# Moved tile regions, halved products and a re-ordered entry in a hybrid decoder layer

## The chip, the cores and the metric

The kernel runs on one core of a Trainium2 chip. The metric is device time in microseconds (us), as the median of several runs. A core has five engines that work from queues of their own: PE (TensorE, the matrix unit, with its weight loads shown apart as PEld), DVE (VectorE), ACT (ScalarE), POOL (GpSimd) and SP (SyncE, here only an issuer of DMAs). Each engine takes its instructions strictly in order; an instruction that has to wait for another engine or for a transfer holds up all behind it.

## The reference

One decoder layer over 512 tokens of width 1024, all in float32, and a last norm:

```python
h = h + 0.5 * swiglu(rmsnorm(h, ffn1_norm), w_gate, w_up, w_down)      # FFN1, inner width 2816
proj = rmsnorm(h, mix_norm) @ w_in                                     # the mix: gMLP and SSD side by side
h = h + concatenate([ya, yb]) @ w_out
h = h + 0.5 * swiglu(rmsnorm(h, ffn2_norm), w_gate, w_up, w_down)      # FFN2
gate = sigmoid(rmsnorm(h, ple_norm) @ ple_w_gate + ple_b_gate)         # the gate
h = h + gate * (p @ ple_w_proj)                                        # p @ ple_w_proj: the embedding
return rmsnorm(h, final_norm)
```

`swiglu(x) = (silu(x @ w_gate) * (x @ w_up)) @ w_down`. `p` is 512 x 256.

## The kernel before, in words

**A product.** Activations lie with the model width over the 128 partitions and the 512 tokens along the free side; a weight block of 128 x 128 is the stationary operand, the activations are the moving one. To keep float32 accuracy on PE, each operand is split into two float32r parts, a high part (`whi`, `xhi`) cast by ACT (L498 for weights) and a low part (`wlo`, `xlo`), the rest, subtracted by DVE (L502). A product is three matmuls into one bank: whi with xhi, whi with xlo, wlo with xhi (L213, L214, L215 in `passes`). Weights arrive by DMA as `raw`, `rawb`, `raw0` or `rawd`.

**Stages.** In order: the embedding p @ ple_proj (two units, steps 0 and 1, L1010), which is written out to DRAM and read back at the end; FFN1; the mix; the projection out; FFN2; the gate; the final norm and the rows out.

**An FFN** has 22 blocks of 128 of the inner width, in eleven groups of two. Group 0 is computed "plainly": four steps (gate and up, each over a lower and an upper half of the width), whose moving operands are the tiles `xfa` and `xfb`, 48 matmuls of 512 columns for the gate and as many for up, 96 in all. Groups 1 to 10 go by a scheme with seven products of 256 columns in place of eight (L712); some of its weights are sums, which are formed by a DMA from POOL that adds to a tile already loaded (L727 and L730 ahead of product 7, L764 for the weights of product 3). Down (`ghi`, `glo` moving, 512 columns) is done in six parts over one or two groups, with weights in `whi` or, from another region, in `whix`.

**The gate** has eight units of 128 of the width: five whole ones of 24 matmuls of 512 columns each (`accumulate` in the loop at L1759) and the last three (`BY_HALF`) by halves of 256 columns, tokens 0 to 255 first, so that the final norm of one half runs beside the products of the other (`gate_half`, 144 matmuls).

**Places.** Tiles come from a base region and from a left and a right region for each stage. `PAD` gives bytes of padding for each; a left region is padded at its start, a right one at its end, from where it grows downwards. In the built programs the tiles begin at these bytes of a partition, modulo 128:

| tile | before | after |
|---|---|---|
| whi, wlo (base) | 0 | 0 |
| xfa, xfb (FFN, left) | 64 | 64 |
| ghi, glo, whix, wlox (FFN, right) | 96 | 0 |
| x of the mix, ya, yb | 0 | 0 |
| x of the gate (ple, left) | 0 | 64 |

Halves of 256 columns lie 1024 bytes apart and so keep the tile's place. The embedding, too, uses ghi and glo of the right region as moving tiles.

**Order.** The first 18 steps follow `ENTRY`, a list written by hand: loadN issues a step's DMAs, splitN its casts and subtractions, productN its matmuls, afterN what is done with the result; N.1 and N.2 are further chains of the step and ":k" its next k pieces. From it and from fixed rules for the rest come the orders of PE, ACT, DVE and SP. POOL's order is not written down; the scheduler places its instructions. Steps 2 to 5 are the plain ones, step 6 is the first L712 product, step 12 a piece of down, and step 13 a product 3 whose weights `rawb` need L764. Before the first real matmul, `WARM` idle matmuls run (L179).

Of the kernel before, what the change touches and what calls it, by code (L numbers as in the profile page):

```python
# [31 lines left out]
P = 128  # L32
T = 512
NC = T // P
D = 1024
ND = D // P
# [6 lines left out]

D_ORDER = tuple(d + i for d in range(NP) for i in (0, NP))
AHEAD = 6
WARM = 10
BY_HALF = 3
LOADS, MIX_LOADS = 6, 4

ENTRY = """  # L50
load0 load1 load1.1 load2 load3 load3.1 split0 load4 split1:1 load5 split1.1:2 split1 split1.1
load6 load6.1 product0 split2 load7 product1 after0 split3 split3.1:6 split4.1:3 split4.2:1
split4.1:1 split4.2:1 split3.1 load8 product2 split4.2:1 after1 split4 split4.1 split4.2:1
split4.2:1 split6.2:1 split4.2 load9 split6.2:1 product3 split5 split5.1 split6.1 split5.2
after4:1 split5.3 product4 split6 after4 split6.2 product5 after4.1 split7 split7.1 load12
product6 split8:1 after5:1 split8 sums9 after6 after5:2 split9:1 split10:1 split10.1:1 after5
product7 split9 load14 product8 after7 split10 split10.1 split14:1 load15 product9 split11
after8 split14 load16 product10 after9 after10 split12 load17 after10.1:1 product11 after11
split13 after10.1 product12 after+10 after11.1:1 after12:1 after11.1 after11.2 product13
after+11 split15 after12 product14 after13:1 split16 after13  # L60
"""

BUFS = {
# [9 lines left out]

PAD = {"sb": 96, "ffn_left": 256, "mix_left": 320, "ple_left": 320, "ffn_right": 0, "mix_right": 96, "ple_right": 0}
HEADS = 16
HD = 64
GROUPS = 2
# [19 lines left out]
def layer_kernel(ctx: ExitStack, tc: tile.TileContext, a: dict, out: bass.AP):  # L99
    nc = tc.nc  # L100
# [76 lines left out]
    ps = sm_ps()  # L177
    for _ in range(WARM):
        nc.tensor.matmul(ps, idle[:, :P], idle, start=True, stop=True)  # L179
    nc.scalar.copy(vec_warm, ones[:, 0:1])  # L180

    upper = sb("upper", (P, P))
    nc.gpsimd.affine_select(
# [26 lines left out]

    def passes(ps, whi, wlo, xhi, xlo, first, last):

        nc.tensor.matmul(ps, whi, xhi, start=first, stop=False)  # L213
        nc.tensor.matmul(ps, whi, xlo, start=False, stop=False)  # L214
        nc.tensor.matmul(ps, wlo, xhi, start=False, stop=last)  # L215

    def accumulate(ps, w, j0, xs, first=True, last=True, tokens=slice(0, T)):

# [464 lines left out]
    class Group:  # L683
# [94 lines left out]
        def plain_steps(self, first):  # L778


            def step(w, i, which, lower):
                w_parts = {}

                def split():
                    return w.split_by_engine(kept=w_parts)

                def product():
                    whi, wlo = w_parts[0]
                    if not lower:
# [182 lines left out]
    def embedding(q):  # L972
        w = Parts()
        ps = []
        raw = sb("g", (P, 2, T)) if q == 0 else None

        def load():
            if q:
                w.load(a["ple_proj"][q])
                return  # L980
            nc.sync.dma_start(raw[:, 0], a["p"][:, 0])
            w.raw = sb(w.tag, (P, 1024))
            for k in range(2):
                c = slice(k * T, (k + 1) * T)
                nc.sync.dma_start(w.raw[:, c], a["ple_proj"][q][:, c])
            nc.sync.dma_start(raw[:, 1], a["p"][:, 1])
            nc.sync.dma_start(vec, a["vecs"])

        def split():
            if q:  # L990
                yield from w.split_by_engine()
                return
            hi, lo = sb("ghi", (P, 2, T), F32R), sb("glo", (P, 2, T), F32R)
            w.take()
            for k in range(2):
                for t, r, u in ((hi[:, k], raw[:, k], lo[:, k]), (w.hi, w.raw, w.lo)):
                    if r is w.raw:
                        t, r, u = (v[:, k * T : (k + 1) * T] for v in (t, r, u))
                    nc.scalar.copy(t, r)
                    nc.vector.tensor_tensor(u, r, t.bitcast(F32), ALU.subtract)  # L1000
            pe.extend((hi[:, k], lo[:, k]) for k in range(2))

        def product():

            ps.extend(acc_ps() if i == 3 else bank("mm", 3) if q else sm_ps() for i in range(4))
            for k, (xhi, xlo) in enumerate(pe):
                for n, (wt, xt) in enumerate(((w.hi, xhi), (w.hi, xlo), (w.lo, xhi))):
                    for i in range(4):
                        c = slice((4 * k + i) * P, (4 * k + i + 1) * P)
                        nc.tensor.matmul(ps[i], wt[:, c], xt, start=k == n == 0, stop=k == 1 and n == 2)  # L1010

        def out():
            for i, tag in enumerate(("embt", "embt", "p7", "u2", "rawd", "rawd", "rawd", "rawd")[4 * q : 4 * q + 4]):
                if tag in ("p7", "u2") or i % 2 == 0:
                    t = sb(tag, (P, 1 if tag in ("p7", "u2") else 2, T))
                    n = 0
                (nc.vector.tensor_copy if i > 1 else nc.scalar.copy)(t[:, n], ps[i])
# [733 lines left out]
    def done(d, ps):  # L1751
# [4 lines left out]
            nc.gpsimd.tensor_tensor(total, total, sq, ALU.add)  # L1756
        gained(d, whole)

    for d in range(ND - BY_HALF):  # L1759
        ps = mm_ps()  # L1760
        accumulate(ps, weights(a["ple_gate"][d], D), 0, x)
        if d == 0:
            tok, first = norm.per_token(D), ps
            continue
        if d == 1:
            r = Norm.on_all(tok)
            done(0, first)
        done(d, ps)
# [138 lines left out]
```

## Time and profile before

| | us |
|---|---|
| median of 3 runs | 1080.93 (1080.79 to 1082.17) |
| the profiled execution | 1080.79 |
| its span | 1079.1 |
| PE busy in it | 1068.1 |
| first matmul of the embedding | 5.65 |
| first plain product of FFN1 | 16.95 |
| first L712 product | 40.55 |
| step 13's first matmul | 59.68 |
| first plain product of FFN2 | 683.42 |
| first matmul of the gate | 1019.72 |

All times in rows are microseconds from the span's start: when an instruction starts, how long it takes, its engine, line and operation, output <- input, and in brackets how long the engine was idle before it and what ended that. Several instructions can be merged in a row (x2, x3). Matmuls overlap, so that a row's duration is longer than the distance to the next start.

### The profile page before, as it was taken

The page shows a single profiled execution, that of the slowest core. Times are in us where ns is not written, and L with a number is a line of the kernel's source. Part 1 is how long each engine was busy: PE and PEld are TensorE (multiplying, and loading weights), DVE is VectorE, ACT ScalarE, POOL GpSimd, SP SyncE. Part 2 cuts the span into 40 slices and gives each one's busy share as a digit, 9 for nine tenths or more (in the row PEclk, how much of TensorE's full clock was granted, in tenths as well). Part 3 has the DMA queues.
Part 4 walks back from the last instruction along what each step waited for, and adds up shares of the span by engine and source line. Part 5 has one row for each costly group of instructions (what it writes and reads, how often), then busy time and mean ns, then how long its engine had stood idle before and what let it go on. Part 6 is the DMA issues. An engine that isn't in the chain of part 4 may idle for free.

```text
span 1079.1 us, 16531 instructions
## 1 busy us (share of the span) xinstructions
PE 1068.1 (99%) x6679; PEld 946.1 (88%) x6679; DVE 778.9 (72%) x1080; ACT 514.9 (48%) x711; POOL 136.5 (13%) x125
## 2 busy tenths in 40 slices
PE   9999999999999999999999999999999999999997
PEld 7999999999998888787888888899999999999887
DVE  7987676666666786766997756688766677677766
ACT  7644444344444455565754334354444434343554
POOL 0100000000001200043233000000000000000411
PEclk9999999999999999999999999999999999999998
DMA  9997776575523332444432333767756676633412
GB/s 346 287 240 186 193 188 183 157 195 159 135 59 120 95 98 81 143 133 135 129 107 77 98 98 98 218 167 200 213 141 168 184 195 177 179 114 107 144 44 79
DMA packets 49885, 163.77 MB, mean 152 GB/s; under 512 B 5648, under 2 KB 5904, under 8 KB 49808
## 3 DMA queue, kind: packets, MB, share of 16 engines
q1 hardware_dynamic: 39872, 129.09, 35.8%
q0 software_dynamic: 8640, 31.46, 16.8%
q10 hardware_dynamic: 1296, 2.16, 0.6%
q8 instruction: 52, 0.85, 0.3%
q14 instruction: 25, 0.20, 0.1%
HBM read 158.43 MB, written 4.26 MB: 151 GB/s over the span
## 4 chain that ended last, share of the span: by engine, by line
PE 89%; DVE 5%; ACT 2%; DMA 1%; issue 1%; SPq 1%; DVEq 0%; ACTq 0%
PE mm L712 20%; PE a L712 15%; PE sm L214 10%; PE sm L213 10%; PE sm L215 10%; PE mm L214 4%; PE mm L213 4%; PE mm L215 4%; PE a L213 3%; PE a L215 3%; PE a L214 3%; DVE wlo L502 1%; DVE tmp L1731 1%; DMA raw<-in_w_in 1%; DMA h<-in_x 1%
## 5 line engine op out<-in xcount | busy, mean ns | idle before, releaser
L498 ACT CAST whi<-raw 128x1024 fp32r<-128x1024 f32 x138 | 144.2, 1046 | 162.0 <-issue 65.0
L502 DVE TENSOR_TENSOR wlo<-raw,whi 128x1024 fp32r<-128x1024 f32 x137 | 172.0, 1255 | 61.0 <-ACT whi L498 59.6
L712 PE MATMUL mm<-xfb,whi 128*128 128x256 f32 x960 | 166.0, 276 | 0.0
L712 PEld LDWEIGHTS mm<-xfb,whi 128*128 128x128 f32 x960 | 145.8, 188 | 1.6
L712 PE MATMUL mm<-xfb,wlo 128*128 128x256 f32 x480 | 132.6, 276 | 0.0
L215 PE MATMUL sm<-ghi,wlox 128*128 128x512 f32 x296 | 116.3, 393 | 0.0
L214 PE MATMUL sm<-glo,whix 128*128 128x512 f32 x296 | 115.9, 391 | 0.0
L213 PE MATMUL sm<-ghi,whix 128*128 128x512 f32 x296 | 115.2, 389 | 0.0
L712 PE MATMUL a<-xfb,whi 128*128 128x256 f32 x640 | 110.9, 276 | 0.0
L712 PEld LDWEIGHTS a<-xfb,whi 128*128 128x128 f32 x640 | 97.7, 188 | 1.9 <-issue 0.2
L712 PEld LDWEIGHTS mm<-xfb,wlo 128*128 128x128 f32 x480 | 90.1, 188 | 0.0
L712 PE MATMUL a<-xfb,wlo 128*128 128x256 f32 x320 | 88.4, 276 | 0.3 <-DVE wlo L502 0.3
L502 DVE TENSOR_TENSOR wlox<-rawd,whix 128x1024 fp32r<-128x1024 f32 (+1 forms) x40 | 45.7, 1142 | 58.8 <-ACT whix L498 58.8
L502 DVE TENSOR_TENSOR wlo<-rawb,whi 128x1024 fp32r<-128x1024 f32 x52 | 63.6, 1223 | 18.9 <-ACT whi L498 18.9
L855 ACT ACTIVATE g<-g 128x512 f32<-128x512 f32 x40 | 25.3, 632 | 106.6 <-DVE g L853 106.6
L727 POOL DMA_DIRECT2D raw<-in_ffn_gu x20 | 17.3, 865 | 401.4 <-DVE h L911 125.3
L498 ACT CAST whi<-rawb 128x1024 fp32r<-128x1024 f32 x52 | 54.3, 1044 | 28.2 <-DVE rawb L722 17.7
L911 DVE SCALAR_TENSOR_TENSOR h<-sm,h 128x512 f32<-128x512 f32 x96 | 63.2, 685 | 5.2 <-PE sm L215 4.6
L215 PEld LDWEIGHTS sm<-ghi,wlox 128*128 128x128 f32 x296 | 55.5, 188 | 11.7
L213 PEld LDWEIGHTS sm<-ghi,whix 128*128 128x128 f32 x296 | 55.6, 188 | 11.0 <-DVE h L911 0.2
L214 PEld LDWEIGHTS sm<-glo,whix 128*128 128x128 f32 x296 | 55.5, 188 | 10.9
L712 PEld LDWEIGHTS a<-xfb,wlo 128*128 128x128 f32 x320 | 60.1, 188 | 0.5 <-DVE wlo L502 0.5
(423 smaller groups left out, 2488.7 us busy)
## 6 DMA issues: line engine op xcount, KB each, us to landing
raw<-in_ffn_gu SPq DMA_DIRECT2D x56, 512.0 KB, 6.0
rawd<-in_ffn_down SPq DMA_DIRECT2D x40, 512.0 KB, 4.0
rawb<-in_ffn_gu SPq DMA_DIRECT2D x32, 512.0 KB, 5.5
raw<-in_ffn_gu POOLq DMA_DIRECT2D x30, 512.0 KB, 5.6
raw<-in_w_in SPq DMA_DIRECT2D x29, 512.0 KB, 3.7
s<-in_ffn_gu SPq DMA_DIRECT2D x20, 512.0 KB, 7.1
s<-in_ffn_gu POOLq DMA_DIRECT2D x20, 512.0 KB, 8.7
raw<-in_w_out SPq DMA_DIRECT2D x16, 512.0 KB, 3.6
```

Source lines behind the costliest of these rows:

```text
L213: nc.tensor.matmul(ps, whi, xhi, start=first, stop=False)
L214: nc.tensor.matmul(ps, whi, xlo, start=False, stop=False)
L215: nc.tensor.matmul(ps, wlo, xhi, start=False, stop=last)
L498: nc.scalar.copy(self.hi[:, : self.n], self.raw[:, : self.n])
L502: nc.vector.tensor_tensor(self.lo[:, :n], self.raw[:, :n], self.hi[:, :n].bitcast(F32), ALU.subtract)
L712: nc.tensor.matmul(o, wt[:, c], xt, start=fresh and p == m == n == 0, stop=last and n == 2, skip_group_check=True,)
L727: nc.gpsimd.dma_start(w21.raw, self.src[0], accum_op=ALU.add)
L855: nc.scalar.activation(t, t, AF.Silu)
L911: nc.vector.scalar_tensor_tensor(h[d], ps[d], 0.5, h[d], ALU.mult, ALU.add)
L1731: engine.tensor_tensor(t, t, emb[d][:, tok], ALU.mult)
```

## The change

It has six parts.

1. `PAD`: `ffn_right` 0 to 96, which moves every tile of the FFNs' right region down by 96 bytes, and `ple_left` 320 to 256, which moves the gate's x by 64 (table above).
2. The plain products: each matmul of 512 columns becomes two of 256 (`passes` once for each half of the tokens). 96 matmuls in each FFN become 192.
3. The gate's five whole units likewise, in `gate_product`: 120 become 240. PE has 312 matmuls more less one idle one.
4. The embedding: the first half of p is asked for by ACT's queue (before it: SP's), ahead of ACT's table load; the first half of the first unit's weights is cast by DVE (before: ACT); the second unit's matmuls go bank by bank, six for each bank, and not pass by pass over four banks.
5. `WARM` 10 to 9.
6. `ENTRY` is another list.

```diff
-WARM = 10
+WARM = 9
...
-load0 load1 load1.1 load2 load3 load3.1 split0 load4 split1:1 load5 split1.1:2 split1 split1.1
+load0 load1 load1.1 load2 load3 load3.1 load4 load5 split0 split1:1 split1.1:3 split1 split1.1
...
-PAD = {"sb": 96, "ffn_left": 256, "mix_left": 320, "ple_left": 320, "ffn_right": 0, "mix_right": 96, "ple_right": 0}
+PAD = {"sb": 96, "ffn_left": 256, "mix_left": 320, "ple_left": 256, "ffn_right": 96, "mix_right": 96, "ple_right": 0}
...
-    nc.scalar.copy(vec_warm, ones[:, 0:1])
...
-        nc.tensor.matmul(ps, whi, xhi, start=first, stop=False)
-        nc.tensor.matmul(ps, whi, xlo, start=False, stop=False)
-        nc.tensor.matmul(ps, wlo, xhi, start=False, stop=last)
+        for n, (w, x) in enumerate(((whi, xhi), (whi, xlo), (wlo, xhi))):
+            nc.tensor.matmul(
+                ps, w, x, start=first and n == 0, stop=last and n == 2, skip_group_check=True
+            )
...
-                            passes(
-                                by_half(ps), whi[:, c], wlo[:, c], t[:, 0:2, 0], t[:, 0:2, 1],
-                                not lower and p == 0, lower and p == len(self.xfs) - 1,
-                            )
+                            for s in range(2):
+                                passes(
+                                    by_half(ps)[:, s], whi[:, c], wlo[:, c], t[:, s, 0], t[:, s, 1],
+                                    not lower and p == s == 0, lower and p == len(self.xfs) - 1 and s == 1,
+                                )
...
-            nc.sync.dma_start(raw[:, 0], a["p"][:, 0])
+            nc.scalar.dma_start(raw[:, 0], a["p"][:, 0])
+            nc.scalar.copy(vec_warm, ones[:, 0:1])
...
-                for t, r, u in ((hi[:, k], raw[:, k], lo[:, k]), (w.hi, w.raw, w.lo)):
-                    if r is w.raw:
-                        t, r, u = (v[:, k * T : (k + 1) * T] for v in (t, r, u))
-                    nc.scalar.copy(t, r)
+                c = slice(k * T, (k + 1) * T)
+                of_p = hi[:, k], raw[:, k], lo[:, k]
+                of_w = w.hi[:, c], w.raw[:, c], w.lo[:, c]
+                nc.scalar.copy(*of_p[:2])
+                (nc.scalar.copy if k else nc.vector.tensor_copy)(*of_w[:2])
+                for t, r, u in (of_p, of_w):
...
-            for k, (xhi, xlo) in enumerate(pe):
-                for n, (wt, xt) in enumerate(((w.hi, xhi), (w.hi, xlo), (w.lo, xhi))):
-                    for i in range(4):
-                        c = slice((4 * k + i) * P, (4 * k + i + 1) * P)
-                        nc.tensor.matmul(ps[i], wt[:, c], xt, start=k == n == 0, stop=k == 1 and n == 2)
+            order = [(k, n, i) for k in range(2) for n in range(3) for i in range(4)]
+            for k, n, i in sorted(order, key=lambda t: t[2]) if q else order:
+                (xhi, xlo), c = pe[k], slice((4 * k + i) * P, (4 * k + i + 1) * P)
+                wt, xt = ((w.hi, xhi), (w.hi, xlo), (w.lo, xhi))[n]
+                nc.tensor.matmul(ps[i], wt[:, c], xt, start=k == n == 0, stop=k == 1 and n == 2)
...
+    def gate_product(ps, w):
+
+        for k, (xhi, xlo) in enumerate(x):
+            for tok in halves:
+                c = slice(k * P, (k + 1) * P)
+                passes(
+                    ps[:, tok], w[0][:, c], w[1][:, c], xhi[:, tok], xlo[:, tok],
+                    k == tok.start == 0, k == ND - 1 and tok.start > 0,
+                )
+
     for d in range(ND - BY_HALF):
         ps = mm_ps()
-        accumulate(ps, weights(a["ple_gate"][d], D), 0, x)
+        gate_product(ps, weights(a["ple_gate"][d], D))
```

The new lines shift line numbers by up to 14; L764 and L727 stay, L1010 becomes L1014, L1017 becomes L1021.

What stands where, at three places. First POOL, whose DMAs add to tiles already loaded, in groups 1 and 2 of FFN1. `rawb_51` before and `rawb_53` after is the tile of step 13; `raw_125` is a tile of group 2's product 7. Before:

```order
L727 DMA raw_62_220<-in_ffn1_gu 128x1024
L730 DMA s1_63_223<-in_ffn1_gu 128x1024
L764 DMA rawb_51_178<-in_ffn1_gu 128x1024
L727 DMA raw_125_610<-in_ffn1_gu 128x1024
L730 DMA s1_126_613<-in_ffn1_gu 128x1024
L727 DMA raw_162_875<-in_ffn1_gu 128x1024
```

And after:

```order
L727 DMA raw_64_225<-in_ffn1_gu 128x1024
L730 DMA s1_65_228<-in_ffn1_gu 128x1024
L727 DMA raw_125_704<-in_ffn1_gu 128x1024
L764 DMA rawb_53_181<-in_ffn1_gu 128x1024
L730 DMA s1_126_707<-in_ffn1_gu 128x1024
L727 DMA raw_162_970<-in_ffn1_gu 128x1024
```

L764 for step 13 and the L727 of raw_125 have changed places.

Second PE, in the embedding's second unit (step 1), whose four banks are mm, mm, mm and a. Before, from the second row of the unit:

```order
L1010 MATMUL mm_66_229<-ghi_41_148,whi_46_162 128x512
L1010 MATMUL mm_67_230<-ghi_41_148,whi_46_162 128x512
L1010 MATMUL a0_68_231<-ghi_41_148,whi_46_162 128x512
L1010 MATMUL mm_65_228<-glo_42_149,whi_46_162 128x512
L1010 MATMUL mm_66_229<-glo_42_149,whi_46_162 128x512
L1010 MATMUL mm_67_230<-glo_42_149,whi_46_162 128x512
L1010 MATMUL a0_68_231<-glo_42_149,whi_46_162 128x512
L1010 MATMUL mm_65_228<-ghi_41_148,wlo_47_163 128x512
```

After, from the second row of the unit:

```order
L1014 MATMUL mm_67_233<-glo_44_152,whi_47_163 128x512
L1014 MATMUL mm_67_233<-ghi_43_151,wlo_48_164 128x512
L1014 MATMUL mm_67_233<-ghi_43_151,whi_47_163 128x512
L1014 MATMUL mm_67_233<-glo_44_152,whi_47_163 128x512
L1014 MATMUL mm_67_233<-ghi_43_151,wlo_48_164 128x512
L1014 MATMUL mm_68_234<-ghi_43_151,whi_47_163 128x512
```

The first matmul with wlo is the unit's third, where it was its ninth, and the first bank is finished after six matmuls, where it was after 21.

Third ACT, where it empties that unit's first two banks into rawd (L1017, after the change L1021). The xfb casts are operands of the upper plain steps. Before:

```order
L498 CAST whi_72_263<-raw0_40_142 128x1024
L596 ACTIVATE glo_74_267<-h_14_102,vec_2_70 128x512
L596 ACTIVATE glo_75_270<-h_16_104,vec_2_70 128x512
L600 CAST xfb_21_109<-glo_74_267 128x2x512
L600 CAST xfb_23_111<-glo_75_270 128x2x512
L629 CAST xfb_21_109<-ghi_76_275 128x512
L629 CAST xfb_23_111<-glo_77_277 128x512
L629 CAST xfb_21_109<-ghi_76_275 128x512
L1017 COPY rawd_81_314<-mm_65_228 128x512
L1017 COPY rawd_81_314<-mm_66_229 128x512
```

And after:

```order
L1021 COPY embt_73_265<-sm_59_192 128x512
L629 CAST xfb_21_107<-ghi_71_261 128x512
L629 CAST xfb_23_109<-glo_72_263 128x512
L498 CAST whi_76_276<-raw0_40_141 128x1024
L600 CAST xfb_21_107<-glo_62_219 128x2x512
L600 CAST xfb_23_109<-glo_63_222 128x2x512
L1021 COPY rawd_81_337<-mm_67_233 128x512
L1021 COPY rawd_81_337<-mm_68_234 128x512
```

One xfb cast fewer stands ahead of the rawd copies, and the two L596 have gone further forward.

Behind the steps of `ENTRY`, ACT, DVE, SP and POOL have the same order as before.

More of the change, by code (lines that the diff above doesn't have):

```diff
@@ L50 @@
 ENTRY = """
-load0 load1 load1.1 load2 load3 load3.1 split0 load4 split1:1 load5 split1.1:2 split1 split1.1
[L52 to L60, printed above, removed]
+load0 load1 load1.1 load2 load3 load3.1 load4 load5 split0 split1:1 split1.1:3 split1 split1.1
+split2 load6 load6.1 product0 split3.1:4 load7 product1 split4.1:2 after0:2 split4.1:1 after0:1
+split4.1:1 after0 split4.2:2 split3 split3.1:2 split4.1:1 split3.1 load8 product2 after1 split4
+split4.1 split6.2:1 split4.2 load9 product3 split5 split5.1 split5.2 split6.2:1 split6.1
+split6.2:1 after4:1 split5.3 product4 after4 split6 split6.2 product5 after4.1 split7 split7.1
+load12 product6 after5:1 split8 after6 sums9 after5:1 split9:1 after5 product7 split10.1:1
+split9 load14 split10.1:1 product8 split10.1:1 after7 split10 split10.1 split14:1 load15
+product9 split11 after8 load16 product10 after9 split12 load17 product11 split13:1 after10
+after10.1:1 split14 after11 after10.1 split13 product12 after+10 after11.1 after11.2 after12:1
+product13 after+11 split15 after12 split16:1 product14 after13:1 split16 after13
 """
```

## The prediction

> **What bounds the kernel now.** I read the page's busy line, then PE's waits, then PE's instructions in order of time, one stretch for each kind of matmul, and last the queues that feed the first steps.
>
> ```profile
> PE 1068.1 (99%) x6679; PEld 946.1 (88%) x6679; DVE 778.9 (72%) x1080; ACT 514.9 (48%) x711; POOL 136.5 (13%) x125
> PE mm L213 <- ACT rawd L1017: 0.5, 1, 0.5
> PE a L712 <- DVE wlo L502: 0.3, 1, 0.3
> ```
>
> PE works nearly always, and its waits are tenths of a microsecond. So the time is the number of matmuls times their pitch (start to start). Pitch, not the busy time of one row, is what to read, since matmuls overlap. Six stretches give it (start, duration):
>
> ```profile
> 683.42 0.39 PE L213 MATMUL sm<-xfa,whi 128*128 128x512 f32 x1
> 694.62 0.95 PE L275 MATMUL sm<-ones,ssum 128*128 128x1 f32 x8
> 991.99 0.39 PE L712 MATMUL mm<-xfb,whi 128*128 128x256 f32 x2
> 997.43 0.39 PE L213 MATMUL sm<-ghi,whi 128*128 128x512 f32 x1
> 1005.57 0.39 PE L215 MATMUL sm<-ghi,wlox 128*128 128x512 f32 x1
> 1008.06 0.39 PE L214 MATMUL sm<-glo,whix 128*128 128x512 f32 x1
> 1008.52 0.39 PE L213 MATMUL sm<-ghi,whi 128*128 128x512 f32 x1
> 1019.72 0.39 PE L213 MATMUL mm<-x,whi 128*128 128x512 f32 x1
> 1025.31 1.05 PE L275 MATMUL sm<-ones,ssum 128*128 128x1 f32 x8
> 1029.07 0.39 PE L213 MATMUL a<-x,whi 128*128 128x512 f32 x1
> 1031.79 0.62 PE L312 MATMUL sm<-tmp,onesr 128*128 128x512 f32 x2
> 1060.08 0.28 PE L213 MATMUL sm<-x,whi 128*128 128x256 f32 x1
> 1062.96 0.28 PE L1786 MATMUL sm<-ones,ssum 128*128 128x1 f32 x2
> ```
>
> 512 columns: 48 of FFN2's plain matmuls in 694.62 - 683.42 = 11.20 us, 233.3 ns each; 48 of down with whi in 1019.72 - 1008.52 = 11.20, 233.3; 11 of down with whix in 2.49, 226.4; 12 of the gate in 2.72, 226.7. 256 columns: 48 of L712 in 5.44, 113.3; 24 of the gate's halves in 2.88, 120.0. Beside the table of places above, one rule fits all six: with 512 columns the moving tile at the stationary tile's place (modulo 128 bytes) gives the short pitch, another place the long one; with 256 columns it is the other way round, 64 bytes apart is short and 0 is long. The table of places after the change says that every 512 column matmul it touches then lies at 0, and every 256 column one at 64.
>
> The sum is made against the profiled execution: 1080.79 us, a span of 1079.1 and 1.7 around it, 0.14 under the median of the runs, 1080.93. All terms but the first are PE's own work on a PE that is never idle beside it.
>
> **1. The entry, to step 13.** Rows of PE, the queues, DVE and ACT in order of time, a bracket giving the idle time before and what ended it:
>
> ```profile
> 11.35 0.86 PE L1010 MATMUL mm<-ghi,whi 128*128 128x512 f32 x3
> 13.22 0.86 PE L1010 MATMUL mm<-ghi,wlo 128*128 128x512 f32 x3
> 22.31 0.40 PE L215 MATMUL sm<-xfa,wlo 128*128 128x512 f32 x1
> 23.20 0.50 PE L213 MATMUL mm<-xfa,whi 128*128 128x512 f32 x1 [0.49 <-ACT rawd L1017]
> 59.68 0.40 PE L712 MATMUL a<-xfb,whi 128*128 128x256 f32 x2
> 59.91 0.28 PE L712 MATMUL a<-xfb,wlo 128*128 128x256 f32 x1
> 0.81 0.39 SPq L981 DMA_DIRECT2D g<-in_p  x1
> 10.92 1.22 DVE L502 TENSOR_TENSOR wlo<-raw,whi 128x1024 fp32r<-128x1024 f32 x1
> 55.99 1.05 ACT L498 CAST whi<-rawb 128x1024 fp32r<-128x1024 f32 x1 [3.20 <-DMA rawb<-in_ffn_gu]
> 57.69 1.22 DVE L502 TENSOR_TENSOR wlo<-rawb,whi 128x1024 fp32r<-128x1024 f32 x1
> 61.82 1.22 DVE L502 TENSOR_TENSOR wlo<-raw,whi 128x1024 fp32r<-128x1024 f32 x1
> 65.41 0.28 PE L712 MATMUL mm<-xfa,wlo 128*128 128x256 f32 x1
> 47.33 0.84 POOL L764 DMA_DIRECT2D rawb<-in_ffn_gu  x1 [16.84 <-DVE wlo L502]
> 49.97 0.86 POOL L727 DMA_DIRECT2D raw<-in_ffn_gu  x1 [1.79 <-DMA raw<-in_ffn_gu]
> 115.28 0.86 POOL L727 DMA_DIRECT2D raw<-in_ffn_gu  x1 [15.52 <-DMA raw<-in_ffn_gu]
> 116.46 0.85 POOL L730 DMA_DIRECT2D s<-in_ffn_gu  x1 [0.33 <-issue]
> ```
>
> POOL's transfers in the view of DMA issues, which ends with the time from issue to landing: the three from 47 to 54 us, then the two from 115 to 117:
>
> ```profile
> rawb<-in_ffn_gu POOLq DMA_DIRECT2D x1, 512.0 KB, 8.6
> raw<-in_ffn_gu POOLq DMA_DIRECT2D x1, 512.0 KB, 8.6
> s<-in_ffn_gu POOLq DMA_DIRECT2D x1, 512.0 KB, 9.2
> ...
> raw<-in_ffn_gu POOLq DMA_DIRECT2D x1, 512.0 KB, 5.6
> s<-in_ffn_gu POOLq DMA_DIRECT2D x1, 512.0 KB, 6.9
> ```
>
> What PE gains by itself: FFN1's 96 plain matmuls as pairs save 96 x 6.6 ns = 0.63. The hole between 22.31 and 23.20 (0.89 where one pitch is 0.23, so 0.66) mostly closes, since the units' banks are finished one by one and ACT can empty rawd's first ones early. p's issue leaves SP (0.39, so ple_proj is asked for 0.4 earlier; ACT's table load now stands behind an issue instead, and what either is worth lies ahead of the wait below). Against it: the second embedding unit needs wlo at its third matmul and not at its ninth. The first wlo matmul would stand some 0.46 behind the unit's start instead of 13.22 - 11.35 = 1.87, and wlo is ready at 10.92 + 1.22 = 12.14, or a few tenths sooner as ACT's cast comes sooner. That is a new wait of 0.3 to 0.8 that eats the earlier start. I take 0.63 + 0.66 - 0.2 = 1.1 us earlier at step 13, were nothing else in the way.
>
> Something is. Step 13's weights are rawb, to which L764 adds by DMA; ACT's cast waited 3.20 us for that landing, and wlo was ready at 57.69 + 1.22 = 58.91, 1.0 before its first use at 59.91. On POOL, L764 used to stand ahead of the second L727; now it stands behind it, and that L727 waits until 49.97 for its own tile's load, which no edit brings sooner (the SP queue's order is otherwise as before). So L764 is issued at 49.97 + 0.86 = 50.83, not 47.33. When does it land? The pair at 115.28 and 116.46 landed at 120.88 and 123.36: the first took 5.6, the second came 2.5 later. By that L727 lands at 55.57 and L764 at 58.05. The ends: as quick as the second of that pair from its own issue, 50.83 + 6.9 = 57.7, or 0.4 less if raw lands sooner, 57.3; as the second of the two in the run before, 49.97 + 8.6 = 58.6. I take 58.05, which lies between them. Then the cast ends at 58.05 + 0.09 + 1.05 = 59.19 and wlo at 60.42: PE's third matmul of step 13 stands at 60.42, not 59.91. What is queued behind the cast and wlo (silu, h, the next wlo) moves by 1.5 too; the next product is not late by it, for its wlo (61.82 + 1.22 = 63.04) stood 2.4 ahead of its use at 65.41, and PE itself is 0.5 later. So the entry's 1.1 is lost and **+0.51** is paid; ends -0.24 (57.3) and +1.1 (58.6). The 12 aligned down matmuls ahead of step 13 are hidden by the same wait.
>
> **2. FFN1's down, last two groups of blocks:** 24 + 48 matmuls with base whi, 72 x 6.6 = 0.48, less what a block pays to settle: 24 gate matmuls took 1025.31 - 1019.72 = 5.59, 0.15 over 24 x 226.7. **-0.34** (ends -0.48, 0).
>
> **3. FFN2's plain:** 96 matmuls of 233.3 as 192 of 113.3: **-0.63**. No row before has a plain pair; the ends are L712's 113.3 (same xfa and xfb, same kind of weights) and the gate halves' 120.0, which would give 96 x 6.7 = +0.64. I take L712's, the row with the same tiles and the same 64 bytes.
>
> The Trainium skill's "TensorE: Matmul & The Clock Gate", section "Back-to-back issue gap", speaks against splitting: beside its columns each isolated matmul costs 2.5 ns, so a pair costs that much more than one of 512. The trace has two of L712 at 226.7, no more than one aligned matmul of 512. By the page's rule the 216 pairs behind step 13 would add an estimated 0.54, and the sum would be 1079.5.
>
> **4. FFN2's down:** 12 + 24 + 48 matmuls x 6.6 = 0.55, less 0.18 to settle: **-0.37** (ends -0.55, 0).
>
> **5. FFN2's one wait:**
>
> ```profile
> 740.83 0.38 PE L712 MATMUL a<-xfb,wlo 128*128 128x256 f32 x1 [0.35 <-DVE wlo L502]
> 739.55 1.23 DVE L502 TENSOR_TENSOR wlo<-raw,whi 128x1024 fp32r<-128x1024 f32 x1 [1.17 <-ACT whi L498]
> ```
>
> PE comes here 0.70 earlier (terms 3 and 4's first 12). The wlo is the end of a chain through DVE and ACT that is partly fed by PE's own earlier products, so a part of it comes earlier too. **+0.2** (ends 0, +0.70).
>
> **6. The gate's five whole units:** 120 matmuls of 226.7 as 240 of 113.3 cost nothing; the settling of the first two (0.15 and some 0.05) goes: **-0.2**; at 120.0 for a half the end is +1.6.
>
> **7. The gate's halves:** 144 matmuls, 120.0 to 113.3 with x moved: 144 x 6.65 = **-0.96** (end 0). The rest of the tail hangs on PE's end.
>
> Sum: 0.51 - 0.34 - 0.63 - 0.37 + 0.2 - 0.2 - 0.96 = -1.79, so 1080.79 - 1.79 = **1079.0 us**.
>
> **The rivals.**
> B, L764 lands in time. If it lands by 56.4, wlo is there when PE comes 1.1 early, term 1 is -1.1 and the time 1080.79 - 3.4 = 1077.4. For it: the 8.6 of the run before was a loaded time, as the 5.6 and 6.9 of the later pair show. Against: from 50.83 that is 5.6 us, the time of a transfer with nothing ahead of it.
>
> C, places don't set the pitch, and halving costs: the long pitch belongs to these tiles for another reason, and a product cut in two pays what the only cut rows of the gate pay, 2 x 120. Then the moves give nothing, FFN2's plain pays +0.64, the gate +1.60, the entry +0.51: 1080.79 + 2.75 = 1083.5, slower. It decides from a pair price of 227.3 ns on (96 and 120 pairs against 49.6 us now, 0.51 beside them). Against it: xfa and xfb themselves show 113.3 in L712, and one tile, ghi, shows 233.3 with whi and 226.4 with whix, so it is the pair of tiles that counts.
> The Trainium skill's "SBUF — State Buffer", section "Who interferes with whom", says that PE never waits on anyone and reads both operands by ports of their own; by it no place should matter, which is this rival; the two pitches of ghi speak against the page.
>
> D, L764 lands as late as the third of the burst did, 52.55 + 9.2 = 61.8, from POOL's row:
>
> ```profile
> 52.55 0.85 POOL L730 DMA_DIRECT2D s<-in_ffn_gu  x1 [1.72 <-DMA s<-in_ffn_gu]
> ```
>
> Then step 13 is 3.7 later than in my sum: 1082.7. From a landing at 59.8 on the gain is gone. For it: all three of that burst took over 8.5, and L764 would stand in its middle.
>
> **How the numbers follow.** This forecast 0.58, B 0.22, C 0.07, D 0.08, others 0.05. A difference under 0.2%, 2.16 us, can't be told from none: faster means under 1078.8, slower over 1083.1. My own case spreads from 1078.2 (57.3 at step 13) to 1080.2, so some two fifths of it lie under 1078.8: faster 0.24 + 0.22 + 0.02 = 0.48; slower, most of C and a part of D, 0.07; same 0.45. The range goes from B to a landing between mine and D's: 1077.1 to 1081.0.
>
> **What would show it.** L712's pitch unchanged, plain, gate and halves all at 113.3, down at 226.7 everywhere: terms 2 to 7. L764 issued after L727 at about 50.8; ACT's cast of rawb near 58.1; a new PE wait on wlo in step 13 of about 1.6 us. Wrong if plain or gate pairs take 240, if down with whi stays at 233, if L764 lands before 57 or after 60, or if a later wait takes the gains back.

## The result, and the profile after

The changed kernel takes 1092.03 us (median of 4 runs, 1090.82 to 1095.70) against 1080.92 (1080.79 to 1082.17) beside it: a ratio of 1.0106 [1.008, 1.0131], 11.1 us slower where 1.9 faster was forecast. The profiled execution is the slowest of the four, 1095.70 us with a span of 1094.0, so the trace has 14.9 us to explain, 3.7 of which the median run does not have.

From the page of the kernel after, the busy line and one group of matmuls, with that group's line on the page of before under it; then, from the view of waits after, PE's:

```profile
PE 1079.2 (99%) x6990; PEld 972.9 (89%) x6990; DVE 781.0 (71%) x1081; ACT 515.0 (47%) x710; POOL 136.6 (12%) x125
L712 PE MATMUL mm<-xfb,whi 128*128 128x256 f32 x960 | 171.4, 280 | 0.0
L712 PE MATMUL mm<-xfb,whi 128*128 128x256 f32 x960 | 166.0, 276 | 0.0
PE a L712 <- ACT whi L498: 2.8, 1, 2.8
PE a L712 <- DVE wlo L502: 1.1, 2, 0.8
PE sm L1800 <- DVE tmp L1741: 0.8, 1, 0.8
```

PE is still never idle but for a few microseconds, so again it is pitch that has grown. Start times of the same work in the two traces, in us from the span's start, show where:

| | before | after | difference | step of it |
|---|---|---|---|---|
| first plain product of FFN1 | 16.95 | 17.25 | +0.30 | +0.30 |
| first L712 product | 40.55 | 39.59 | -0.96 | -1.26 |
| step 13 | 59.68 | 61.64 | +1.96 | +2.92 |
| the product behind step 13 | 65.18 | 69.87 | +4.69 | +2.73 |
| last L712 product of FFN1 | 327.38 | 337.60 | +10.22 | +5.53 |
| first plain product of FFN2 | 683.42 | 693.22 | +9.80 | -0.42 |
| first L712 product of FFN2 | 707.17 | 717.00 | +9.83 | +0.03 |
| last L712 product of FFN2 | 994.71 | 1009.77 | +15.06 | +5.23 |
| first matmul of the gate | 1019.72 | 1034.36 | +14.64 | -0.42 |
| end of the span | 1079.1 | 1094.0 | +14.9 | +0.26 |

Two things carry it: a slow creep of 5.5 and 5.2 us through the L712 products of both FFNs, and 5.65 us around step 13.

**The creep.** PE's instructions in order of time near the end of FFN2, at the place where the prediction read 48 of L712 in 5.44 us. After:

```profile
1006.26 0.39 PE L213 MATMUL sm<-ghi,whix 128*128 128x512 f32 x1
1006.49 0.39 PE L213 MATMUL sm<-glo,whix 128*128 128x512 f32 x1
1006.72 0.39 PE L213 MATMUL sm<-ghi,wlox 128*128 128x512 f32 x1
1006.94 0.40 PE L712 MATMUL mm<-xfb,whi 128*128 128x256 f32 x2
1007.18 0.28 PE L712 MATMUL mm<-xfb,wlo 128*128 128x256 f32 x1
...
1009.77 0.40 PE L712 MATMUL a<-xfb,whi 128*128 128x256 f32 x2
...
1012.60 0.39 PE L213 MATMUL sm<-ghi,whi 128*128 128x512 f32 x1
```

48 of L712 now take 1012.60 - 1006.94 = 5.66 us, 117.9 ns each and not 113.3, although neither xfa, xfb nor the weights have another address. In the whole trace 3072 of the 3744 matmuls with xfa or xfb and 256 columns are at 118 (counted by products of 24, each by its median pitch). I call the step from the last matmul of down to the first of L712 the hand-over. Down's rows ahead of the same place before, its first ones and its last:

```profile
986.73 0.40 PE L214 MATMUL sm<-glo,whix 128*128 128x512 f32 x1
986.96 0.40 PE L215 MATMUL sm<-ghi,wlox 128*128 128x512 f32 x1
...
991.30 0.39 PE L213 MATMUL sm<-ghi,whix 128*128 128x512 f32 x1
991.53 0.39 PE L214 MATMUL sm<-glo,whix 128*128 128x512 f32 x1
991.75 0.40 PE L215 MATMUL sm<-ghi,wlox 128*128 128x512 f32 x1
```

The difference is in the last 512 column matmul. Before, it is uneven, that is, its pitch is not that of its neighbours: it is 0.40 long and 237 ns from its successor (unrounded), where they have 227. After, it is as even as the rest, 227. The other sign is on the other side of the block: before, down's first matmuls behind L712 are uneven too (986.73, 986.96: 0.40), after they run at 226.7 from the first. What these rows show holds nearly everywhere: the trace of before has 40 hand-overs, and in 37 of them the last pitch is 236 or 237 ns and the product behind it is at 113; after, 37 have 226 or 227 and 118 behind it.

**Step 13.** These are rows of POOL, ACT, DVE and PE in order of time, after:

```profile
50.72 0.84 POOL L727 DMA_DIRECT2D raw<-in_ffn_gu  x1 [20.73 <-DVE wlo L502]
51.26 1.19 POOL L764 DMA_DIRECT2D rawb<-in_ffn_gu  x1
60.54 1.04 ACT L498 CAST whi<-rawb 128x1024 fp32r<-128x1024 f32 x1 [8.71 <-DMA rawb<-in_ffn_gu]
61.62 1.23 DVE L502 TENSOR_TENSOR wlo<-rawb,whi 128x1024 fp32r<-128x1024 f32 x1 [4.81 <-ACT whi L498]
61.64 0.50 PE L712 MATMUL a<-xfb,whi 128*128 128x256 f32 x2 [2.82 <-ACT whi L498]
62.90 0.38 PE L712 MATMUL a<-xfb,wlo 128*128 128x256 f32 x1 [0.76 <-DVE wlo L502]
```

L764's transfer lands 9.2 us after its issue. The issue was late too, since L727 ahead of it waits for the load of its own tile, which landed 7.7 us after its issue at 42.44; the same load took 6.5 us before. L727 goes out 0.55 us behind that landing, as it does in experiments 2 and 10; the DVE instruction in its bracket ended in between. PE waits 2.82 us for whi, does two matmuls, and waits 0.76 for wlo. Then it works at half speed: windows of 2 us, with the granted clock in the column behind the five engines:

```profile
62.00:64.00 2.00, 1.24 (x9) 1.10 (x8) 2.00 (x4) 0.12 (x1) 0.00 (x0) 0.88 1.02 325
64.00:66.00 2.00, 2.00 (x12) 2.00 (x11) 2.00 (x5) 1.92 (x3) 0.00 (x0) 0.50 1.02 418
66.00:68.00 2.00, 2.00 (x11) 1.88 (x11) 2.00 (x3) 0.59 (x1) 0.00 (x0) 0.77 1.02 420
68.00:70.00 2.00, 2.00 (x11) 1.63 (x11) 2.00 (x3) 1.21 (x2) 1.30 (x2) 1.00 0.22 49
```

The clock's shortfall is 2 x (0.12 + 0.50 + 0.23) = 1.70 us of work, some 3.4 us at half clock. The first wlo matmul stands 62.90 - 61.64 = 1.26 behind the first with whi, 1.03 more than two pitches; 1.70 + 1.03 = 2.73 is the step behind step 13 in the table. The Trainium skill's "TensorE: Matmul & The Clock Gate", section "What's actually happening", has the clock halved after an idle window of about 3.4 us and restored after a busy one. The 3.4 us at half clock agree with it; the fall came sooner than that, since no idle stretch here is longer than 2.82 us and two matmuls stand between it and the 0.76.

**The rest.** FFN2's plain products, now pairs:

```profile
693.22 0.40 PE L213 MATMUL sm<-xfa,whi 128*128 128x256 f32 x2
693.46 0.28 PE L213 MATMUL sm<-xfa,wlo 128*128 128x256 f32 x1
...
698.88 0.40 PE L213 MATMUL mm<-xfa,whi 128*128 128x256 f32 x2
```

The first 48 take 5.66 us, 117.9 each; two of them are 235.8 where one whole matmul was 233.3 before. FFN1's plain products, pairs as well, are at 113 in all eight of their products of 24. In the gate, the halves of the last three units do reach the short pitch, 24 in 2.72 us:

```profile
1073.93 0.39 PE L213 MATMUL sm<-x,whi 128*128 128x256 f32 x2
...
1076.65 0.39 PE L213 MATMUL sm<-x,whi 128*128 128x256 f32 x2
```

And yet the end came no sooner.

### The profile page after: what moved, and what is told of

Same layout as the page of the kernel before. It is cut to its first block, busy times and chain, and to the rows that moved or that the text cites. A ratio compares the mean times of both kernels' runs of the same rounds, so it can differ in the third digit from the quotient of the medians.

```text
span 1094.0 us, 17159 instructions
## 1 busy us (share of the span) xinstructions
PE 1079.2 (99%) x6990; PEld 972.9 (89%) x6990; DVE 781.0 (71%) x1081; ACT 515.0 (47%) x710; POOL 136.6 (12%) x125
## 4 chain that ended last, share of the span: by engine, by line
PE 85%; DVE 6%; DMA 4%; ACT 2%; issue 2%; SPq 0%; DVEq 0%; POOL 0%; ACTq 0%
PE sm L213 29%; PE mm L712 19%; PE a L712 15%; PE mm L213 11%; PE a L213 8%; DMA emb_dram<-rawd 1%; DMA h<-in_x 1%; DVE wlo L502 1%; ACT whi L498 1%; DMA rawb<-in_ffn_gu 1%; DVE tmp L1735 1%; DMA rawd<-in_ffn_down 1%; PE sm L275 1%; PE sm L1620 1%; PE sm L1448 0%
## 5 line engine op out<-in xcount | busy, mean ns | idle before, releaser
L712 PE MATMUL mm<-xfb,whi 128*128 128x256 f32 x960 | 171.4, 280 | 0.0
L712 PEld LDWEIGHTS mm<-xfb,whi 128*128 128x128 f32 x960 | 147.5, 188 | 1.4
L712 PE MATMUL mm<-xfb,wlo 128*128 128x256 f32 x480 | 134.6, 280 | 0.0
L712 PE MATMUL a<-xfb,whi 128*128 128x256 f32 x640 | 116.2, 283 | 2.8 <-ACT whi L498 2.8
L712 PEld LDWEIGHTS a<-xfb,whi 128*128 128x128 f32 x640 | 100.1, 190 | 5.1 <-ACT whi L498 3.2
L712 PEld LDWEIGHTS mm<-xfb,wlo 128*128 128x128 f32 x480 | 91.9, 191 | 0.0
L712 PE MATMUL a<-xfb,wlo 128*128 128x256 f32 x320 | 90.7, 283 | 1.1 <-DVE wlo L502 1.1
L213 PE MATMUL sm<-x,whi 128*128 128x512 f32 (+1 forms) x304 | 82.1, 359 | 0.0
L727 POOL DMA_DIRECT2D raw<-in_ffn_gu x20 | 17.3, 864 | 422.6 <-DMA raw<-in_ffn_gu 116.1
```

Source lines behind the costliest of these rows:

```text
L213: nc.tensor.matmul(ps, w, x, start=first and n == 0, stop=last and n == 2, skip_group_check=True)
L712: nc.tensor.matmul(o, wt[:, c], xt, start=fresh and p == m == n == 0, stop=last and n == 2, skip_group_check=True,)
L727: nc.gpsimd.dma_start(w21.raw, self.src[0], accum_op=ALU.add)
```

## The experiments

There were three theories at the start. Hand-over: L712's pitch depends on how the stream before it ended, and `ffn_right` alone made that end even (the recorded texts call it the pace theory). Stall: step 13's late weights, or the clock that fell there, set off the long pitch. Halving: the 256 column pairs of the plain products, which have the same two tiles, bring it.

**1. `ffn_right` alone**, in the kernel before:

```diff
-PAD = {..., "ffn_right": 0, ...}
+PAD = {..., "ffn_right": 96, ...}
```

> The kernel before with ffn_right at 96 and nothing else. Pace theory: PE keeps the step it was in; a stream of 512 column matmuls at place 0 that has settled at 226.7 ns hands L712 a phase in which it runs at 117.8 ns and not 113.3, until PE runs empty for a moment. Then down at place 0 alone does the harm: L712 at 117.8 in most groups, down at 226.7, the entry as before, 1086 to 1094 us (13 us if all but 450 of the 3360 L712 matmuls are slow, less 0.7 for down). Stall theory: the long wait in step 13, which also cost the clock, put PE into the slow step; without that wait L712 stays at 113.3 and the time is 1080.2.

1090.61 us (1090.28 to 1090.81) against 1081.07: 1.0089 [1.0072, 1.0105]. L712's group on its page:

```profile
L712 PE MATMUL mm<-xfb,whi 128*128 128x256 f32 x960 | 171.5, 280 | 0.0
```

These are the same 280 ns as after, where 276 stood before; 3024 of 3360 are at 118. From start to start, all L712 matmuls took 394.70 us where they took 381.89 before, +12.8; down gained 1.0 with whi (39.48 to 38.51) and 2.1 with whix (203.42 to 201.32). Together this is +9.7; the span grew by 9.9. Of 40 hand-overs, 39 now have a last pitch of 226 or 227 and 118 behind it. So far the hand-over theory holds: one number of the change is nearly all of the loss.

**2. The change with `ffn_right` at 0 again:**

```diff
-PAD = {..., "ffn_right": 96, ...}
+PAD = {..., "ffn_right": 0, ...}
```

> The changed kernel with ffn_right back at 0; the late L764 stays. Pace theory: L712 at 113.3 behind every down block; step 13 and the one behind it still 4.7 us late; the gate's halves 0.96 better: 1083.5 to 1085.5 us. Stall theory: the wait of step 13 is there, so L712 runs at 117.8 for the rest of FFN1 at least: 1088 us or more.

1082.33 us (1080.34 to 1084.74, 10 runs) against 1081.07: 1.0011 [1.0002, 1.002], below the 1083.5 to 1085.5 expected. L712 is back at 113 (3288 of 3360). What is left is the entry and the gate: in this profile the cast of rawb starts at 57.37 and PE waits 0.53 in step 13, less than the expectation took from the changed kernel's profile; but the runs scatter over 4.4 us where the kernel before scatters over 1.3.

**3. The change with whole plain products:**

```diff
-for s in range(2):
-    passes(by_half(ps)[:, s], ..., t[:, s, 0], t[:, s, 1], ...)
+passes(by_half(ps), ..., t[:, 0:2, 0], t[:, 0:2, 1], ...)
```

> The changed kernel with the plain products of both FFNs whole again (512 columns), which also puts POOL's L764 back ahead of the second L727. Both theories: no wait above 0.3 us in step 13, and L712 about 1 us earlier than before there. Pace theory: L712 still at 117.8 in most groups, for ffn_right is still 96: 1086 to 1093 us. Stall theory: L712 at 113.3 throughout, 1078 to 1079.5 us.

1090.32 us (1089.88 to 1090.65): 1.0086 [1.0071, 1.0101]. With whole products the scheduler's POOL order is the old one, L764 first; PE has no wait in step 13; and L712 is at 118 all the same, in 3024 of its 3360 matmuls. Stall and halving fall as causes of the creep.

**4. Both, `ffn_right` at 0 and whole plain products:**

> The changed kernel with ffn_right at 0 and the plain products whole: what is left is the entry's new order, p on ACT's queue, the gate in halves and its x moved. Both theories: no late L764 and L712 at 113.3. Entry -0.4 to -1.1, the gate's halves -0.96, its whole units 0 to +0.5 (how a stream of 256 columns starts behind down is open): 1078.5 to 1080.0 us.

1081.23 us (1080.34 to 1081.66): 1.0002 [0.9992, 1.0011]. It missed: what is left of the change (the entry, the gate) should have won 1.1 to 2.6 us and won nothing. The first L712 product came 0.09 later than before, not earlier; and the gate's end came no sooner, which experiment 11 takes up.

So the question became which hand-over is even. Down ends on tiles of the right region, at its place, and L712 begins on whi, at 0: before, 96 bytes apart, after, none. By that, any other place of the region should keep L712 short.

**5 and 6. Two other places for the right region**, in the kernel before: `ffn_right` 32 puts ghi and whix at 64, 64 puts them at 32.

```diff
-PAD = {..., "ffn_right": 0, ...}
+PAD = {..., "ffn_right": 32, ...}
```

> The kernel before with ffn_right at 32, so that ghi, glo, whix and wlox lie at 64. Pace theory, with the change of the stationary tile's place at the hand-over as what breaks the step (whix at 64, then whi at 0; before it was 96, then 0): down with whix settles at 226.7, down with base whi stays at 233.3, L712 is at 113.3 behind both, 1080.4 to 1081.8 us. If it was not that change but something of 96 alone: L712 at 117.8 behind the whix blocks, 1088 us or more.

1091.49 us (1091.11 to 1091.87): 1.0098 [1.0078, 1.0118].

```diff
-PAD = {..., "ffn_right": 0, ...}
+PAD = {..., "ffn_right": 64, ...}
```

> The kernel before with ffn_right at 64, so that ghi, glo, whix and wlox lie at 32. Pace theory as for 32: L712 at 113.3, down with base whi at 233.3, 1080.4 to 1081.8 us. Only place 0, where no tile changes its place at the hand-over, should lose. If it was something of 96 alone: 1088 us or more.

1080.66 us (1080.40 to 1080.93): 0.9998 [0.9987, 1.0008]. L712's group, first of `ffn_right` 32, then of 64:

```profile
L712 PE MATMUL mm<-xfb,whi 128*128 128x256 f32 x960 | 171.5, 281 | 0.0
```

```profile
L712 PE MATMUL mm<-xfb,whi 128*128 128x256 f32 x960 | 166.5, 277 | 0.0
```

The first was a miss: place 64 was to be short and is as long as 0. With the tiles at 32 and 96 the hand-over is uneven (a last pitch of 235, and of 237) and L712 short; at 0 and 64 it is even (225 to 227) and L712 long. So, as far as these four places show, a difference of 64 bytes at the hand-over counts as none. The pitch of down itself is another matter: with whi it is 226.7 at place 0, 233.4 at 32 and 96, and 229 at 64, where 233.3 was expected: a third value, which the prediction's rule of two does not have.

**7. `ffn_right` 96, and the unevenness put back by other means:** the last matmul of each step of down (wlo with xhi) as two of 256 columns.

```diff
-nc.tensor.matmul(ps, wlo, xhi, start=False, stop=last)
+for s in (slice(0, HT), slice(HT, T)) if cut else (slice(None),):
+    nc.tensor.matmul(ps[:, s], wlo, xhi[:, s], ...)
...
-accumulate(ps[d], (w.hi, w.lo), ..., end == len(gs_))
+accumulate(ps[d], (w.hi, w.lo), ..., end == len(gs_), cut=d == ds[-1])
```

> The kernel before with ffn_right at 96, and in each of down's steps the very last matmul (wlo with xhi) as two of 256 columns. These two lie at place 0, where the gate's halves ran at 120 and not 113.3. Pace theory: the two are an uneven place in the stream and break the step, so that L712 comes back to 113.3 while down keeps 226.7: 1080.9 - 3.2 for down (216 base and 888 whix matmuls) + 44 x 0.013 for the cuts + some 0.6 for settling = 1078.9, 1078 to 1080 us. If the step outlives them (the pace belongs to the tiles' places alone): 117.8, 1090 to 1092 us.

1079.66 us (1079.28 to 1079.94, 10 runs) against 1080.87: 0.9989 [0.9979, 0.9998], faster than before. PE's instructions at the end of a part of down (L715 is L712 there):

```profile
293.67 0.39 PE L213 MATMUL sm<-ghi,whix 128*128 128x512 f32 x1
293.89 0.39 PE L214 MATMUL sm<-glo,whix 128*128 128x512 f32 x1
294.12 0.40 PE L216 MATMUL sm<-ghi,wlox 128*128 128x256 f32 x2
294.35 0.40 PE L715 MATMUL mm<-xfb,whi 128*128 128x256 f32 x2
294.59 0.28 PE L715 MATMUL mm<-xfb,wlo 128*128 128x256 f32 x1
294.71 0.39 PE L715 MATMUL mm<-xfb,whi 128*128 128x256 f32 x2
...
299.81 0.39 PE L715 MATMUL mm<-xfa,whi 128*128 128x256 f32 x2
```

The cut matmul and the first three of L715 are uneven; then 45 take 299.81 - 294.71 = 5.10 us, 113.3 each. 3216 of 3360 are at 113, with ghi and whix at place 0 and down at 227. The edit moves no tile against experiment 1; 50 of down's 1056 matmuls are cut, and some 11 us are gone.

**8. `ffn_right` 96, the last three matmuls of down in another order** (whi xhi, wlo xhi, whi xlo):

```diff
-three[0], three[1], three[2]
+three[0], three[2], three[1]  # in the last step of each part of down
```

> The kernel before with ffn_right at 96, and in each of down's steps the last three matmuls in the order whi xhi, wlo xhi, whi xlo. The same places, the same columns and as many matmuls; only the last weights before L712 are whi and not wlo. Pace theory: nothing uneven comes in, L712 stays at 117.8 and the time at 1090.6 us. If what counts is which weight tile L712 follows, L712 is at 113.3 and the time 1078 to 1080 us.

1091.20 us (1091.13 to 1091.28): 1.0095 [1.0075, 1.0115], L712 at 118. Which weight comes last makes no difference; what 1, 5, 6, 7 and 8 have in common is that L712 is short where the end of down is uneven and long where it is even.

**9 and 10. The changed kernel with the cut of 7**, once with POOL's order that of the program (L764 first), once with the scheduler's (L764 second, as after):

```diff
-ORDERED = {mybir.EngineType.PE, ..., mybir.EngineType.SP}
+ORDERED = {mybir.EngineType.PE, ..., mybir.EngineType.SP, mybir.EngineType.Pool}
```

> The changed kernel with the cut in down's last matmul (as in the kernel before with ffn_right 96 and the cut, which took 1079.7 us) and with POOL's DMAs in the order in which the program writes them, so that L764 for step 13 stands ahead of the second L727 again. Queue theory (the late landing is POOL's order): no wait over 0.3 us in step 13, step 13 some 0.95 us earlier than before, runs within 1.5 us of each other, 1078.5 to 1080 us. Rival (the wait comes from the new entry itself, whatever POOL's order): step 13 waits 1 to 3 us as in the changed kernel. Open: later L727s now stand behind an L764 too and may be late.

1079.14 us (1078.51 to 1080.01) against 1080.99: 0.9984 [0.9975, 0.9993].

> The changed kernel with the cut alone. Pace theory: L712 back at 113.3 but for what follows the projection out. What is left against the kernel before is the late L764 (0 to 4.7 us, and different from run to run) and the gate (0.3 to 0.5): 1080 to 1085 us, runs several us apart. If L712 in the changed kernel has another cause than down's hand-over: 1088 us or more.

1079.86 us (1078.85 to 1080.65): 0.999 [0.9981, 0.9999]. POOL and ACT in order of time, first with L764 ahead (L770 and L733 are L764 and L727 in both):

```profile
46.22 0.84 POOL L770 DMA_DIRECT2D rawb<-in_ffn_gu  x1 [16.83 <-DVE wlo L508]
48.08 0.86 POOL L733 DMA_DIRECT2D raw<-in_ffn_gu  x1 [1.01 <-DMA raw<-in_ffn_gu]
53.57 1.05 ACT L504 CAST whi<-rawb 128x1024 fp32r<-128x1024 f32 x1 [2.04 <-DMA rawb<-in_ffn_gu]
```

and with it behind:

```profile
48.64 0.84 POOL L733 DMA_DIRECT2D raw<-in_ffn_gu  x1 [18.89 <-DMA raw<-in_ffn_gu]
49.17 1.19 POOL L770 DMA_DIRECT2D rawb<-in_ffn_gu  x1
57.05 1.05 ACT L504 CAST whi<-rawb 128x1024 fp32r<-128x1024 f32 x1 [4.82 <-DMA rawb<-in_ffn_gu]
```

The swap on POOL costs 3.5 us in the cast (53.57 to 57.05), and here 0.7 us of time, within the scatter of both. The profile of experiment 10 has no wait of PE in step 13, and its time missed the expectation on the good side. In the profile of the changed kernel the same order cost 5.65, since there L727 went out at 50.72 and the cast began at 60.54. What the late L764 costs is thus between 0 and some 6 us, run by run. With the cut alone (experiment 10) the changed kernel's median is 12.2 us lower; how much of that is the cut's and how much an earlier landing of L764, the two times don't tell.

**11. The gate's part alone**, in the kernel before: `ple_left` 256 and `gate_product` for the whole units.

> The kernel before with ple_left at 256 and the gate's whole units in halves; nothing else. Chain theory: from the gate's third whole unit on, the end is set by a chain through DVE and ACT that starts when that unit is done, and not by PE; a shorter pitch of the halves is worth nothing, and the chain starts as much later as the first three units take longer (pairs behind a break start at 117 to 120): 0 to +0.6, 1080.9 to 1081.5 us. The prediction's terms 6 and 7 (PE's pace sets the end): -1.16, 1079.7 us.

1081.18 us (nine runs from 1080.97 to 1081.62, and one of 6019.11, of which no trace was kept) against 1080.99: 1.0002 [0.9993, 1.0011]. The chain that ended last, where it leaves the gate's matmuls: before (with the one place where it comes back to PE), after, and in this experiment.

```profile
1037.39 0.24 PE mm L214
1037.66 1.05 ACT whi L498
...
1071.04 0.84 PE sm L1786 x6
```

```profile
1047.23 5.35 PE mm L213 x47
1052.60 1.05 ACT whi L498
```

```profile
1032.71 5.35 PE mm L214 x47
1038.08 1.05 ACT whi L499
```

From that cast to the end of the span are 1079.1 - 1037.66 = 41.4 us, 1094.0 - 1052.60 = 41.4 and 1079.4 - 1038.08 = 41.3: a chain of ACT and DVE (tmp, h, wlo) which starts when PE ends the gate's third unit, and in which no matmul of the gate lies; PE has 0.84 us of it, six small matmuls of the final norm. The 144 halves stand beside it. Their shorter pitch only lets PE wait longer: in experiment 11 the last gate products start 0.5 earlier against before, and PE ends 0.4 later. The time is what that chain allows, and not the 1079.7 of a PE that sets the end.

**12. What had helped so far, together:** the changed kernel with the cut, whole plain products and the gate as before (`ple_left` 320, whole units by `accumulate`).

> The changed kernel with the cut, the plain products whole (which keeps L764 ahead of L727) and the gate as before, its x at place 0. It joins what the runs so far showed to gain: down at place 0 with the cut (1079.7), and the entry's 0.75 us that the kernel with whole plain products had at its first L712. 1078.5 to 1079.4 us; 1079.7 or more if the entry's gain is lost later.

1078.89 us in the median of 12 runs, eleven of them from 1078.54 to 1079.71 and one at 1092.55; ratio 0.9993 [0.9972, 1.0014], the interval widened by the lone run, for which there is no trace. By its median it is the lowest, 2.1 us under the kernel before, but only 0.25 under experiment 9, which is less than either scatters; the clear interval is experiment 9's.

## Why the prediction was wrong

The step that failed is the reading "one rule fits all six": that a pitch belongs to the places of two tiles. From it came "L712's pitch unchanged", so that the largest stream of all, 3360 matmuls, stood in the sum at nothing. The six rows were right, but they were six settled states. A pitch also depends on what ran before. A stream of 256 columns at 64 bytes apart has two states, 113.3 and 117.8. Behind an uneven end of down it is in the first, behind an even stream of 226.7 in the second, where it stays over the products that follow. Not every break ends that: in experiment 1 a first pitch of 189 ns, at 734.34, did not end the long state, and one of 348 in the product at 745.63 did. Before, the misplaced right region made nearly every hand-over uneven. The move to place 0 took 3.1 us out of down and the unevenness with it, at a price of 12.8 in L712. The trace of before had the sign in its rows: the 0.40 at 991.75 and 986.73, and the "settling" that terms 2, 4 and 6 subtract. I priced the settling as a small loss of down's and did not ask what L712 had from it.

By terms:

1. *The entry, +0.51.* The mechanism was right (L764 behind L727, a new wait on rawb in step 13), the size not. Issue 51.26 and not 50.83; landing 60.4 and not 58.05, nearer to rival D's 61.8. The landing took 9.2 us from the issue, where I had 7.2. Two later runs of the same order had their cast at 57.05 and 57.37, near my early end of 57.3. What the sum lacked is the clock, which falls when PE has waited that long: 1.70 us more. The entry itself was 0.96 earlier at the first L712 product, of 1.1 forecast; in experiments 3, 4 and 12, 0.73 earlier, 0.09 later and 0.41 earlier.
2. and 4. *Down, -0.34 and -0.37.* The sign was right and the size short: 226.7 nearly everywhere, and 3.1 us gained in experiment 1, since the settling behind each L712 block goes as well, which I had charged to the change.
3. *FFN2's plain, -0.63.* Failed: +0.03. The pairs fell into the 117.8 state, coming from an even stream (ya with whi). It is neither L712's 113.3 nor the halves' 120.0. FFN1's pairs, with the same tiles and as many, did run at 113, so the choice of row was right for one of two places.
5. *FFN2's one wait, +0.2.* It is 0.39 us long after and 0.35 before. PE did not come early, so this tested nothing.
6. *The gate's whole units, -0.2.* Failed: from the gate's first matmul to the chain's first cast it is 1052.60 - 1034.36 = 18.24 us, against 1037.66 - 1019.72 = 17.94 before, +0.30. The first 96 halves ran in the long state.
7. *The gate's halves, -0.96.* The pitch came as forecast, 113.3. "The rest of the tail hangs on PE's end" was wrong: it hangs on 41.4 us of work that is nearly all ACT's and DVE's. PE's busy line of 99% hid that, and the chain that ended last, read in its last 60 us of before, would have shown it.

The rivals: C had the side but not the reason. In the short state halving costs nothing: two of 113.3 are one of 226.7, and the 2.5 ns for each matmul of the Trainium skill's "Back-to-back issue gap" do not show. D came nearest as to the landing in the profiled run, 60.4 against its 61.8 and my 58.05. Without the right region's move, in experiment 2, the time was 1082.33; that is 1.3 us of a loss of 11.1, and its closeness to D's 1082.7 is chance, since the cast of rawb began at 57.37 there. B fell as to its landing: in the three profiles of this order L764 landed at 60.4, 57.3 and 57.0, none by 56.4, though the last was in time for PE (experiment 10).

In one point the trace goes on speaking against the Trainium skill's "SBUF — State Buffer", section "Who interferes with whom", by which PE waits on no one and reads its operands independently: experiments 1 and 6 differ in the place of one region by 32 bytes, and in time by 10 us.

Still open: in what the two states of the 256 column stream differ inside PE, and how large an unevenness has to be to change the state (no view shows it); why the load of L727's tile took 7.7 us in the profile of the changed kernel and 5.7 and 6.1 in those of experiments 2 and 10, where L727 went out at 48.6 and not at 50.7; and the lone run of 1092.55 in experiment 12. Its excess of 13.7 is near what L712 loses in the long state, but its granted clock is 0.947 where the other eleven runs, and all of experiment 1 with its long L712, have 0.997 to 0.999; so that state alone does not explain it.

## What to carry to other kernels

Where one engine is full, price every long stream by the state it runs in and not by its operands alone: before a stream is made "clean", ask what the next stream had from its irregular end, and try the one edit alone. A term counts only if it lies on the chain that ends last; 99% busy does not mean that an engine's end sets the end. And when a hand-placed order leaves one queue to a scheduler, look at that queue again after each change.

## What was unexpected in the hardware

The pitch of a matmul stream has memory. With the same L712 instructions, addresses and clock, 256 column matmuls run at 113.3 or at 117.8 ns for thousands of matmuls, over blocks and hand-overs, and one cut matmul at the end of each step of down decides which (experiments 1 and 7). In the long state the loads of wlo are longer too, as the view of one tile shows, minimum, median and maximum in ns, before and after:

```profile
L712 PEld LDWEIGHTS mm<-xfb,wlo x480: 187/188/188, 43.4 to 994.5; 128*128 128x128 f32 x160
```

```profile
L712 PEld LDWEIGHTS mm<-xfb,wlo x480: 187/192/192, 42.4 to 1009.5; 128*128 128x128 f32 x160
```

The clock is a second thing: two waits of 2.82 and 0.76 us cost PE another 1.70 us of clock behind them, nearly half of the waits themselves. It shows in one profile only, the one with a wait this long.
